# Two-block transformer kernel: differential queries and keys computed with tokens stationary and turned by VectorE and moves; which queues issue the moves

## The chip, the cores and the metric

The kernel runs on one core of a Trainium2 chip. The metric is the device time of one execution in microseconds; the median of three runs stands for the kernel.

## What is computed

The reference chains two layers over 256 tokens of 2048 channels, all in float32: a sliding-window attention layer, and a layer with a latent attention branch (MLA, 16 heads), a differential attention branch (8 heads, two 128-wide query/key pairs each), gates for both, and a gated feed-forward network. The change is in the differential branch:

```
dq, dk, dv = columns of h @ w_in                       # 2048 columns each
q = dq.reshape(b, s, 8, 2, 128); k likewise; v = dv.reshape(b, s, 8, 256)
sc = einsum('bqhmd,bkhmd->bhmqk', q, k) / sqrt(128) - slope_h * |i - j|   # chunk mask of 64
p = softmax(sc);  a = p[:, :, 0] - lam * p[:, :, 1]
o = rmsnorm(einsum('bhqk,bkhd->bqhd', a, v)) * (1 - lambda_init)
merged = g0 * (y_mla @ w_mla_proj) + g1 * (o @ w_diff_proj)
x = x + merged @ w_out;   then   x = x + (silu(h2 @ w_gate) * (h2 @ w_up)) @ w_down
```

## The kernel before

All weights lie in one array `w` of 340 chunks of 1 MB, in the order in which they are used: a chunk is 16 weight tiles of 128 x 128. SyncE (SP) loads them in that order into four buffers `w_raw` (line 54). Every half chunk is split into a high and a low part of type float32r: ScalarE (ACT) casts the high one (`w_hi`, line 85), VectorE (DVE) subtracts (`w_lo`, line 86), four buffers each. Activations are split in the same way. A product is then three float32r products: high x high, high x low, low x high. All matmuls are issued by `mm` (line 209).

There are two forms of the big products. `gemm` (line 330) holds a weight tile stationary and sends activations through: `w_hi` against the 512 columns (high and low) of one k, `w_lo` against the 256 high ones; the result has channels on partitions. `gemm_nat` (line 389) holds 128 tokens stationary and sends four weight tiles through: for each k and each of two token halves `nat3` (line 378) issues three matmuls of 512 columns; the result has tokens on partitions, in two PSUM banks.

The differential branch is a loop over u = 0 to 3, two heads each (lines 977 to 996). In a step, eight blocks of `gemm("dqk", ...)` make four blocks of queries and four of keys, channels on partitions; each is summed from its PSUM halves and scaled by `scaled` (line 420: one ScalarE copy, two VectorE operations of 128 x 256). `gemm_nat("dv", ...)` makes the values. Then `attend_d` (line 919) is put into an interleaver. In step 0 the gates 0 to 3 and the `mla` projections follow; after the loop come the gates 4 to 7, `diff`, `out`, the feed-forward products `ffn` and `down`, all by `gemm_nat`.

The interleaver (lines 127 to 168) sets where attention stands in program order. The big products report the tiles that they have taken; after `every` tiles there is a tick, and a tick advances one generator up to its next `yield n`, which says after how many ticks it may go on (`apart` if it says nothing). During the differential loop from u = 0's end, `every` is 8 and `apart` 3; from the gates' end on `every` is 16. Program order is what the framework's list scheduler starts from; on each engine the instructions then run in one fixed order, and an instruction that waits holds up all behind it.

Some tensors are turned (transposed) without TensorE. VectorE transposes blocks of 32 x 32 (`nc.vector.transpose`), and `moved` (line 447) carries the blocks between partition groups with 16 small DMAs, four for each of four column groups `a`. Their issuing engine is GpSimd (POOL) unless a `queue` is given; with `fourth` given, the four of `a == 3` go to that queue. Before the change, the moves of probabilities (`prob_t`, line 468) have `fourth=nc.sync`; those of the turned outputs (`o_t`, line 917), of the merged, and of the ffn activations (`turned`, line 456) are all GpSimd's, as are the loads of the gates' bias rows (`row`, line 487, from line 950); the moves of the residual (`x1n`, lines 965 to 974) are all SyncE's. `split_turned` (line 471) makes the high and low copies of turned activations on ScalarE and VectorE, 5 ticks after it is first advanced.

Weight columns for results that will be turned are permuted on the host by `_quarters` (line 1153), so that after the 32 x 32 transposes and moves the channels stand in order.

Of the kernel before, what the change touches and what calls it, by code (L numbers as in the profile page):

```python
# [171 lines left out]
def block_kernel(ctx, tc, order, w, x01, xt, bc, rw, cst, out):  # L172
# [29 lines left out]
    def half(t, i):  # L202
        return t[:, (i % 2) * S:(i % 2) * S + S]
# [217 lines left out]
        total(o, ps)  # L421
        tt(o, o, rb, ALU.mult)

    def scores(parts, ps):

        n = len(parts)
        for j, (q, k) in enumerate(parts):
            mm(ps[:, 0:P], q[:, 0:P], k[:, 0:P], j == 0, False)
        for j, (q, k) in enumerate(parts):
            mm(ps[:, P:384], q[:, P:S], k[:, 0:S], False, j == n - 1)  # L430

    def exps(ps, table, scale, negmax, sums, init, rows=None):

        t = unit("prob")[:, 0:384]
# [18 lines left out]
                    out=o[32 * b:32 * b + 32, a * n:a * n + n], in_=tr[32 * a:32 * a + 32, b * n:b * n + n])  # L453
        return o

    def turned(z, queue=nc.gpsimd):

        tr = unit("turn")
        nc.vector.transpose(out=tr, in_=z)  # L459
        return moved(tr, unit("turned"), queue)  # L460

    def turned_probs(p):

# [4 lines left out]
        d = moved(tr, wide("prob_t"), fourth=nc.sync).rearrange("p (a e k i) -> p e k a i", a=4, e=2, k=3)  # L468
        return [d[:, e] for e in range(2)]

    def split_turned(acts, k0, parts):

        yield 5
        hls = []
        for t in parts:
            t = t.rearrange("p (a g i) -> p g a i", a=4, g=4)
            make = unit2 if acts is act and k0 < 8 else unit
            hi, lo = make("t_hi", F32R), make("t_lo", F32R)
            oh, ol = (o.rearrange("p (g a i) -> p g a i", a=4, g=4) for o in (hi, lo))
            nc.scalar.copy(out=oh, in_=t)  # L480
            tt(ol, t, oh.bitcast(F32), ALU.subtract)
            hls.append((hi, lo))
        for g in range(4):
            q = slice(g * P, g * P + P)
            acts[k0 + g] = [(hi[:, q], lo[:, q]) for hi, lo in hls]
# [383 lines left out]
    tab_d = unit("tab_d")[:, 0:384]  # L869
    nc.scalar.dma_start(out=tab_d, in_=cst[:, C_DD:C_DD + 384])  # L870

    def probs_d(head, q, k):
        negmax, sums, rec = sm("negmax"), sm("sums"), sm("rec")
        slope = 2.0 ** -(head + 1)
        bias = unit("bias")[:, 0:384]
        nc.scalar.activation(out=bias, in_=tab_d, func=AF.Copy, scale=slope / scale_d)
        p = []
        for m in range(2):
            ps = bank("s")
            scores([(half(q, m), half(k, m))], ps)  # L880
            p.append(exps(ps, bias, scale_d, negmax[:, 2 * m:2 * m + 2], sums[:, 2 * m:2 * m + 2], BIG))
        nc.vector.reciprocal(out=rec, in_=sums)
        nc.vector.tensor_scalar(out=rec[:, 2:4], in0=rec[:, 2:4], scalar1=neglam, scalar2=None, op0=ALU.mult)
        for qb, (a, b) in enumerate(((0, P), (P, 384))):
            nc.scalar.activation(out=p[1][:, a:b], in_=p[1][:, a:b], func=AF.Copy, scale=rec[:, 2 + qb:3 + qb])
            nc.vector.scalar_tensor_tensor(out=p[0][:, a:b], in0=p[0][:, a:b], scalar=rec[:, qb:qb + 1],
                                           in1=p[1][:, a:b], op0=ALU.mult, op1=ALU.add)
        return p[0]
# [20 lines left out]
    def turned_values(o, r):  # L909

        tr = unit("o_tr")
        to = tr.rearrange("p (b d q i) -> p q d b i", b=4, d=2, q=2)
        for qb in range(2):
            nc.vector.tensor_scalar(out=half(o, qb), in0=half(o, qb), scalar1=r[:, qb:qb + 1], scalar2=None,
                                    op0=ALU.mult)
            nc.vector.transpose(out=to[:, qb], in_=half(o, qb).rearrange("p (d b j) -> p d b j", d=2, b=4))
        return moved(tr, unit("o_t"))

    def attend_d(u, q, k, v):
        heads = (2 * u, 2 * u + 1)  # L920
        p = []
        for e, head in enumerate(heads):
            p.append(probs_d(head, q[e], k[e]))
            yield
        pts = turned_probs(p)
        yield 9
        ms = sm("ms_d")
        os = []
        for e in range(2):
            os.append(values_d(pts[e], [(half(a, e), half(b, e)) for a, b in v], ms[:, 2 * e:2 * e + 2]))  # L930
            yield
        r = rstd(ms, S)
        yield
        ots = [turned_values(o, r[:, 2 * e:2 * e + 2]) for e, o in enumerate(os)]
        for e, head in enumerate(heads):
            yield 8
            ot = ots[e].rearrange("p (a d q i) -> p d q a i", a=4, d=2, q=2)
            for d in range(2):
                y = unit(f"y_d{2 * head + d}", F32R)
                g = g_d[:, d:d + 1]  # L940
                for tb in range(2):
                    hi, lo = (half(y, i)[:, tb * P:tb * P + P].rearrange("p (a i) -> p a i", a=4) for i in range(2))
                    nc.scalar.activation(out=hi, in_=ot[:, d, tb], func=AF.Copy, scale=g)
                    nc.vector.scalar_tensor_tensor(out=lo, in0=ot[:, d, tb], scalar=g, in1=hi.bitcast(F32),
                                                   op0=ALU.mult, op1=ALU.subtract)
                y_d[2 * head + d] = y

    def gate(i):

        b = row(R_GATE, i)  # L950
        o = []
        for tb, ps in enumerate(gemm_nat("gate", i * 512, h)):
            t = unit("gate")
            nc.vector.scalar_tensor_tensor(out=t, in0=ps, scalar=r_2[:, tb:tb + 1], in1=b, op0=ALU.mult, op1=ALU.add)
            nc.scalar.activation(out=t, in_=t, func=AF.Tanh, scale=0.5)
            o.append(t)
        return o
# [7 lines left out]
    def turn_residual():  # L965
        for cb in range(4):
            for tb in range(2):
                yield 8
                tr = unit("turn")
                for i in range(4):  # L970
                    nc.vector.transpose(
                        out=tr.rearrange("p (a m j) -> p a m j", a=4, m=4)[:, :, i, :],
                        in_=x1[4 * cb + i][:, tb * P:tb * P + P].rearrange("p (a j) -> p a j", a=4))
                x1n.append(moved(tr, unit("x1n"), nc.sync))

    mer = []
    for u in range(4):
        qk = []
        for c in (0, 16):
            for i in range(4):  # L980
                ps = gemm("dqk", c + 4 * u + i, h)
                if i % 2 == 0:
                    qk.append(unit("qk_d"))
                scaled(half(qk[-1], i), ps, rb_2)
        pp = gemm_nat("dv", u * 512, h)
        v = []
        for tb in range(2):
# [5 lines left out]
        if u == 0:  # L993
            between.drain()
            between.every, between.apart = 8, 3
        between.add(attend_d(u, qk[0:2], qk[2:4], v))
        if u == 0:
            between.add(turn_residual())
            for i in range(4):
# [51 lines left out]
    for u in range(KF // 4):  # L1051
# [11 lines left out]
            pu = gemm_nat("ffn", DFF + u * 512, h)  # L1063
        for tb, ps in enumerate(pu):
            tt(parts[tb], ps, parts[tb], ALU.mult)
            parts[tb] = turned(parts[tb])
        between.add(split_turned(act, 4 * u, parts))

    tot = sm("tot", 10)
    fgt = []  # L1070
# [91 lines left out]
def _matrices(i):  # L1162

    pairs = []
    for j in range(16):
# [11 lines left out]
        "out_a": i["w_out_a"][0][pairs],  # L1177
        "in_2": in_2[:, :1280],
        "kpe": np.concatenate([kpe, kpe], axis=1),
        "dqk": in_2[:, 1344:5440],  # L1180
        "dv": in_2[:, 5440:7488],
        "gate": in_2[:, 7488:][:, _quarters(2 * D)],
        "uq": np.concatenate([uq[:, :, :128].reshape(768, -1), uq[:, :, 128:].reshape(768, -1)], axis=1),
# [44 lines left out]
```

## Time and profile before

| | |
|---|---|
| time, median of 3 runs | 1982.64 us (1982.47 to 1982.7) |
| the profiled execution | 1981.54 us |
| its span, first to last instruction | 1979.8 us |
| mean granted TensorE clock | 0.998 |
| ScalarE, VectorE busy | 997.5 us, 1247.0 us |
| DMA, mean over the span | 199 GB/s |

In the rows below, a line of a timeline has the start in us, the duration in us, engine, line of the kernel, operation, output tile <- input tiles, shape, number of instructions merged, and in brackets how long the engine idled before it and what ended that. POOLq and SPq are the issuing sequencers. Rows by tile have durations in ns (least, median, most) and the first and last start. Rows of DMA issues end with the median us from issue to landing. Matmul records overlap, since TensorE is pipelined; the pitch is read from the starts.

### The profile page before, as it was taken

Reading aid. Unit: us, or ns where it says so; the run is one execution under the profiler, and the core shown is the slowest. Engines: PE = TensorE matmul, PEld = TensorE weight load, DVE = VectorE, ACT = ScalarE, POOL = GpSimd, SP = SyncE. Lnnn points to the kernel's source line nnn. Section 1 sums busy time; section 2 is a strip of 40 time slices with the busy share of each in tenths; the row PEclk is TensorE's granted clock in tenths of the full one; section 3 lists DMA queues with packets and bytes.
Section 4 is the critical chain, followed back from the end, with each engine's and each line's share of the span. In section 5 each row is a group of like instructions: output and inputs, shape, how many; then the busy total and the mean of one; then the engine's idle time right before and its main releaser. Section 6 shows DMA issues by size and latency. Waiting matters only on the chain. (4 is left out here: it accounts for less than half of the span.)

```text
span 1979.8 us, 27202 instructions
## 1 busy us (share of the span) xinstructions
PE 1960.2 (99%) x9756; PEld 1648.5 (83%) x9756; DVE 1247.0 (63%) x1960; ACT 997.5 (50%) x1577; POOL 526.9 (27%) x1069
## 2 busy tenths in 40 slices
PE   9999999999999999999999999999999999999998
PEld 8888888888888888888888888887888888888886
DVE  7889766888856655566666666655555555544453
ACT  6677664756645444455554445544444444434443
POOL 0555200014311300014043565433444333330000
PEclk9999999999999999999999999999999999999999
DMA  8565554445455555555556665655556565565552
GB/s 304 186 211 190 187 212 160 173 152 197 159 202 198 170 222 223 198 180 186 200 200 229 210 215 190 238 208 194 207 207 210 204 211 204 202 224 192 193 192 105
DMA packets 100793, 393.16 MB, mean 199 GB/s; under 512 B 27248, under 2 KB 53104, under 8 KB 57520
## 3 DMA queue, kind: packets, MB, share of 16 engines
q1 hardware_dynamic: 65184, 366.17, 51.4%
q0 software_dynamic: 34320, 23.27, 4.2%
q10 hardware_dynamic: 1152, 1.97, 0.3%
q8 instruction: 77, 1.26, 0.3%
q14 instruction: 60, 0.49, 0.1%
HBM read 364.03 MB, written 2.10 MB: 185 GB/s over the span
## 5 line engine op out<-in xcount | busy, mean ns | idle before, releaser
L86 DVE TENSOR_TENSOR w_lo<-w_raw,w_hi 128x1024 fp32r<-128x1024 f32 (+1 forms) x677 | 821.2, 1218 | 556.8 <-ACT w_hi L85 552.3
L85 ACT CAST w_hi<-w_raw 128x1024 fp32r<-128x1024 f32 (+1 forms) x677 | 705.0, 1046 | 707.3 <-PE ps_g L209 632.5
L209 PE MATMUL ps_g<-w_lo,t_hi 128*128 128x512 f32 x1176 | 457.6, 389 | 0.8 <-DVE w_lo L86 0.8
L209 PE MATMUL ps_g<-w_hi,t_hi 128*128 128x512 f32 x1176 | 457.6, 389 | 0.6 <-ACT w_hi L85 0.6
L209 PE MATMUL ps_g<-w_hi,t_lo 128*128 128x512 f32 x1176 | 457.4, 389 | 0.0
L452 POOL DMA_DIRECT2D turned<-turn x576 | 281.7, 497 | 394.5 <-DVE turn L459 169.5
L209 PE MATMUL ps_g<-h,w_hi 128*128 128x512 f32 x1160 | 283.7, 393 | 3.1 <-ACT w_hi L85 2.8
L452 POOL DMA_DIRECT2D prob_t<-prob_tr x336 | 164.7, 498 | 397.5 <-DVE prob_tr L467 274.2
L209 PEld LDWEIGHTS ps_g<-w_hi,t_hi 128*128 128x128 f32 x1176 | 220.8, 188 | 46.8 <-ACT w_hi L85 1.0
L209 PEld LDWEIGHTS ps_g<-w_lo,t_hi 128*128 128x128 f32 x1176 | 220.8, 188 | 46.6 <-DVE w_lo L86 1.1
L209 PEld LDWEIGHTS ps_g<-w_hi,t_lo 128*128 128x128 f32 x1176 | 220.8, 188 | 45.9
L209 PEld LDWEIGHTS ps_g<-h,w_hi 128*128 128x128 f32 x1160 | 212.0, 188 | 47.8 <-ACT w_hi L85 3.4
L209 PE MATMUL ps_g<-w_hi,h 128*128 128x512 f32 x768 | 240.9, 391 | 0.0
L209 PEld LDWEIGHTS ps_g<-w_hi,h 128*128 128x128 f32 x768 | 144.2, 188 | 29.9
L209 PEld LDWEIGHTS ps_g<-h,w_lo 128*128 128x128 f32 x1160 | 150.2, 191 | 9.7 <-issue 3.0
L209 PE MATMUL ps_g<-h,w_lo 128*128 128x256 f32 x1160 | 155.2, 284 | 0.0
L209 PE MATMUL ps_g<-w_lo,h 128*128 128x512 f32 x384 | 149.7, 390 | 0.9 <-DVE w_lo L86 0.7
L290 POOL TENSOR_TENSOR rstd<-ms,mhalf 128x2 f32<-128x2 f32 (+1 forms) x10 | 9.2, 920 | 358.6 <-DVE ms L285 341.0
L209 PEld LDWEIGHTS ps_g<-w_lo,h 128*128 128x128 f32 x384 | 72.1, 188 | 16.2 <-DVE w_lo L86 1.6
L452 POOL DMA_DIRECT2D o_t<-o_tr x128 | 62.8, 498 | 63.0 <-issue 24.8
L209 PE MATMUL ps_g<-w_hi,y_m 128*128 128x512 f32 x256 | 79.5, 389 | 0.0
L209 PE MATMUL ps_g<-w_hi,y_d 128*128 128x512 f32 x256 | 78.9, 389 | 0.0
(240 smaller groups left out, 1799.6 us busy)
## 6 DMA issues: line engine op xcount, KB each, us to landing
w_raw<-w SPq DMA_DIRECT2D x337, 1024.0 KB, 5.0
turned<-turn POOLq DMA_DIRECT2D x576, 16.0 KB, 4.0
prob_t<-prob_tr POOLq DMA_DIRECT2D x336, 24.0 KB, 3.6
row<-rw POOLq DMA_DIRECT2D x12, 256.0 KB, 3.7
prob_t<-prob_tr SPq DMA_DIRECT2D x112, 24.0 KB, 2.9
w_raw<-w SPq DMA_DIRECT2D x5, 512.0 KB, 7.6
x1n<-turn SPq DMA_DIRECT2D x128, 16.0 KB, 1.8
o_t<-o_tr POOLq DMA_DIRECT2D x128, 16.0 KB, 3.8
```

Of the source, the lines that this page charges most:

```text
L85: a = nc.scalar.copy(out=hi[:, q], in_=src[:, q])
L86: b = nc.vector.tensor_tensor(out=lo[:, q], in0=src[:, q], in1=hi.bitcast(F32)[:, q], op=ALU.subtract)
L209: nc.tensor.matmul(out=o, lhsT=a, rhs=b, start=start, stop=stop, skip_group_check=True)
L290: nc.gpsimd.tensor_tensor(out=r, in0=t, in1=mhalf[:, 0:n], op=ALU.pow)
L452: (fourth if fourth and a == 3 else queue).dma_start(out=o[32 * b:32 * b + 32, a * n:a * n + n], in_=tr[32 * a:32 * a + 32, b * n:b * n + n])
```

## The change

Queries and keys of the differential branch are computed by `gemm_nat`, four weight tiles of one k at a time, and evicted by one scaled ScalarE copy per token half. Each 128 x 512 result is turned by VectorE and 16 moves, of which 4 go to SyncE. A new function `dense_d`, run as the first part of `attend_d`, copies the turned queries and keys on ScalarE into the layout that the scores read. The helper `scores` goes; its two products per pair are written out in `probs_d`. The ticks of `attend_d` are set anew: 2, 1, 2, 1, 8, 1, 1, 1, 8, 1 in place of 3, 3, 9, 3, 3, 3, 8, 8.

The moves of `o_t` and of the ffn activations also give a fourth to SyncE. Those of `x1n`, before all on SyncE, go three quarters to GpSimd. The bias rows of the gates are loaded by SyncE. In the ffn, `split_turned` waits 7 ticks in place of 5. The columns of `dqk` are permuted by `_quarters`.

```diff
-    def turned(z, queue=nc.gpsimd):
+    def turned(z, queue=nc.gpsimd, fourth=None):
         tr = unit("turn")
         nc.vector.transpose(out=tr, in_=z)
-        return moved(tr, unit("turned"), queue)
+        return moved(tr, unit("turned"), queue, fourth)
...
-    def split_turned(acts, k0, parts):
-        yield 5
+    def split_turned(acts, k0, parts, wait=5):
+        yield wait
...
-    def probs_d(head, q, k):
+    def dense_d(q, k):
+        qs, ks = [], [unit("k_d") for _ in range(2)]
+        for tb in range(2):
+            t = unit("q_d")
+            nc.scalar.copy(out=t.rearrange("p (g a i) -> p g a i", a=4, g=4),
+                           in_=q[tb].rearrange("p (a g i) -> p g a i", a=4, g=4))
+            qs.append(t)
+            for e in range(2):
+                nc.scalar.copy(out=ks[e].rearrange("p (g t a i) -> p t g a i", g=2, t=2, a=4)[:, tb],
+                               in_=k[tb].rearrange("p (a g i) -> p g a i", a=4, g=4)[:, 2 * e:2 * e + 2])
+        return qs, ks
+
+    def probs_d(head, e, qs, ks):
...
             ps = bank("s")
-            scores([(half(q, m), half(k, m))], ps)
+            qm = [q[:, (2 * e + m) * P:(2 * e + m) * P + P] for q in qs]
+            mm(ps[:, 0:P], qm[0], ks[e][:, m * S:m * S + P], True, False)
+            mm(ps[:, P:384], qm[1], half(ks[e], m), False, True)
...
-        return moved(tr, unit("o_t"))
+        return moved(tr, unit("o_t"), fourth=nc.sync)
 
     def attend_d(u, q, k, v):
         heads = (2 * u, 2 * u + 1)
+        yield 2
+        qs, ks = dense_d(q, k)
+        yield 1
         p = []
         for e, head in enumerate(heads):
-            p.append(probs_d(head, q[e], k[e]))
-            yield
+            p.append(probs_d(head, e, qs, ks))
+            yield 2 - e
         pts = turned_probs(p)
-        yield 9
+        yield 8
...
-            yield
+            yield 1
         r = rstd(ms, S)
-        yield
+        yield 1
         ots = [turned_values(o, r[:, 2 * e:2 * e + 2]) for e, o in enumerate(os)]
         for e, head in enumerate(heads):
-            yield 8
+            yield 1 if e else 8
...
-        b = row(R_GATE, i)
+        b = row(R_GATE, i, nc.sync)
...
-                x1n.append(moved(tr, unit("x1n"), nc.sync))
+                x1n.append(moved(tr, unit("x1n"), fourth=nc.sync))
...
         for c in (0, 16):
-            for i in range(4):
-                ps = gemm("dqk", c + 4 * u + i, h)
-                if i % 2 == 0:
-                    qk.append(unit("qk_d"))
-                scaled(half(qk[-1], i), ps, rb_2)
+            parts = []
+            for tb, ps in enumerate(gemm_nat("dqk", (c + 4 * u) * P, h)):
+                z = unit("qk_d")
+                nc.scalar.activation(out=z, in_=ps, func=AF.Copy, scale=r_2[:, tb:tb + 1])
+                parts.append(turned(z, fourth=nc.sync))
+            qk.append(parts)
...
-        between.add(attend_d(u, qk[0:2], qk[2:4], v))
+        between.add(attend_d(u, qk[0], qk[1], v))
...
-            parts[tb] = turned(parts[tb])
-        between.add(split_turned(act, 4 * u, parts))
+            parts[tb] = turned(parts[tb], fourth=nc.sync)
+        between.add(split_turned(act, 4 * u, parts, 7))
...
-        "dqk": in_2[:, 1344:5440],
+        "dqk": in_2[:, 1344:5440][:, _quarters(2 * D)],
```

More of the change, by code (lines that the diff above doesn't have):

```diff
@@ L422, in scaled @@
         tt(o, o, rb, ALU.mult)
[L424 to L430, printed above, removed]
     def exps(ps, table, scale, negmax, sums, init, rows=None):
```

## The prediction

> **What bounds the kernel now.** I read the page first, then the chain of waits in order of time, then the timelines of TensorE, ScalarE, SyncE and GpSimd around the places where TensorE idled, and last the rows by tile for durations. Page and chain:
>
> ```profile
> span 1979.8 us, 27202 instructions
> PE 1960.2 (99%) x9756; PEld 1648.5 (83%) x9756; DVE 1247.0 (63%) x1960; ACT 997.5 (50%) x1577; POOL 526.9 (27%) x1069
> ...
> 1368.55 595.77 PE ps_g L209 x2627
> ```
>
> The span is TensorE's: 99% busy, and the last 596 us of the chain are one unbroken run of matmuls. That run is made by `gemm_nat` alone, 512 columns each, so one of these costs 595.77 / 2627 = 226.8 ns from start to start. Every other engine has room on the average. So the change can act in two ways: by another number of nanoseconds of matmul, and by stalls of TensorE that go or come. Vector, scalar and move work that causes no stall costs nothing.
>
> **Matmul time.** The rewritten part is the 32 blocks of `gemm("dqk", ...)`, 16 weight tiles each. In TensorE's timeline one block reads:
>
> ```profile
> 783.33 3.82 PE L209 MATMUL ps_g<-h,w_hi 128*128 128x512 f32 x16
> 786.99 2.08 PE L209 MATMUL ps_g<-h,w_lo 128*128 128x256 f32 x16
> 788.90 3.82 PE L209 MATMUL ps_g<-h,w_hi 128*128 128x512 f32 x16
> ```
>
> The starts matter, not the durations, which overlap: 16 matmuls of 512 columns take 786.99 - 783.33 = 3.66 us (228.8 ns each), 16 of 256 take 788.90 - 786.99 = 1.91 us (119.4 ns), a block 5.57 us (5.565 over two blocks, by the starts). [...] With tokens stationary, `gemm_nat` sends the same columns as 96 matmuls of 512 for four blocks (6 for each of 16 k), where there were 64 of 512 and 64 of 256. That is 24 x 226.8 ns = 5.44 us a block. The gain is 0.12 us a block, times 32 = 3.9 us.
>
> [...]
>
> The scores are the same four products per head with the same widths, so I cost them at zero; they are now issued inside the same streams as before.
>
> **Stalls of TensorE that the change touches.** From the dqk blocks on, TensorE's timeline shows idle time before four matmuls, at three places:
>
> ```profile
> 779.47 2.11 PE L209 MATMUL ps_g<-h,w_hi 128*128 128x512 f32 x8 [2.24 <-ACT w_hi L85]
> ...
> 1024.46 0.50 PE L209 MATMUL ps_g<-w_lo,h 128*128 128x512 f32 x1 [0.73 <-DVE w_lo L86]
> ...
> 1367.29 0.49 PE L209 MATMUL ps_g<-w_hi,t_hi 128*128 128x512 f32 x1 [0.58 <-ACT w_hi L85]
> 1368.55 0.50 PE L209 MATMUL ps_g<-w_lo,t_hi 128*128 128x512 f32 x1 [0.77 <-DVE w_lo L86]
> ```
>
> They add to 4.32 us. The record of a matmul lasts longer (0.39) than its pitch (0.227), which hides 0.16 us of each: 4 x 0.16 = 0.65, together 5.0 us. In each the weights' split came late; why, the other engines show:
>
> ```profile
> 751.68 21.50 SPq L452 DMA_DIRECT2D x1n<-turn  x32
> 773.28 15.09 SPq L54 DMA_DIRECT2D w_raw<-w  x7
> ...
> 778.38 2.00 ACT L85 CAST w_hi<-w_raw 128x1024 fp32r<-128x1024 f32 x2 [11.06 <-DMA w_raw<-w]
> ...
> 1021.68 0.51 ACT L894 CAST a_hi<-prob_t 128x384 fp32r<-128x384 f32 x1 [7.91 <-DMA row<-rw]
> ...
> 1355.36 0.62 ACT L480 CAST t_hi<-turned 128x512 fp32r<-128x512 f32 x1 [6.60 <-DMA turned<-turn]
> ...
> 1364.52 0.62 ACT L480 CAST t_hi<-turned 128x512 fp32r<-128x512 f32 x1 [5.69 <-DMA turned<-turn]
> ```
>
> First: SyncE issued 32 moves of `x1n` in one run of 21.5 us; the weight loads stood behind them. Now three quarters go to GpSimd and 8 of such 32 stay on SyncE, a run of about 5.4 us. As 21.5 us overran the weights' lead by only 2.4 us, the lead is about 19 us and 5.4 us is covered. Second: ScalarE stood 7.9 us at the copy of turned probabilities. Third: it stood at the copies of turned ffn activations (6.6 and 5.7 us). A ScalarE wait blocks the casts of weights queued behind it, and TensorE runs dry when the wait exceeds ScalarE's lead: 7.91 us of wait cost 0.73 + 0.16 = 0.9 us, so the lead is about 7.0 us. For the second place GpSimd's timeline says what was slow:
>
> ```profile
> 1010.18 3.91 POOL L452 DMA_DIRECT2D prob_t<-prob_tr  x8 [1.05 <-DMA o_t<-o_tr]
> 1015.08 1.96 POOL L452 DMA_DIRECT2D prob_t<-prob_tr  x4 [0.99 <-DMA prob_t<-prob_tr]
> 1017.03 1.09 POOL L490 DMA_DIRECT2D row<-rw  x2
> ...
> 1056.11 4.43 POOL L452 DMA_DIRECT2D o_t<-o_tr  x9 [9.31 <-issue]
> ...
> 1072.78 2.94 POOL L452 DMA_DIRECT2D o_t<-o_tr  x6 [1.41 <-DMA o_t<-o_tr]
> ```
>
> The probabilities queued behind `o_t` moves and ahead of bias rows. A long run of moves also waits for its own landings: 32 moves of `o_t` took 1075.72 - 1056.11 = 19.6 us, 0.61 us each. After the change a run of 32 is 24 on GpSimd, 14.7 us, and the bias rows are off its queue. The ffn copies wait 7 ticks of 16 tiles instead of 5: two ticks are 2 x 24 x 226.8 ns = 10.9 us more, above the 5.7 us by which they were late. I take all 5.0 us as gone; at the least it is the first alone, 2.4 us.
>
> **The other terms, and what hides them.**
>
> ```profile
> L417 ACT COPY qk_d<-ps_g x32: 348/372/379, 520.1 to 958.8; 128x256 f32<-128x256 f32 x32
> L212 DVE TENSOR_TENSOR qk_d<-qk_d,ps_g x32: 383/420/422, 520.5 to 959.2; 128x256 f32<-128x256 f32 x32
> L212 DVE TENSOR_TENSOR qk_d<-qk_d,rb_kr x32: 382/425/426, 521.4 to 959.6; 128x256 f32<-128x256 f32 x32
> ...
> L989 ACT ACTIVATE v_hi<-ps_g,r x8: 687/689/691, 590.2 to 982.7; 128x512 fp32r<-128x512 f32 x8
> ...
> L459 DVE STREAM_TRANSPOSE turn<-ffn x22: 701/703/706, 1294.0 to 1732.9; 128x512 f32<-128x512 f32 x22
> ...
> L480 ACT CAST t_hi<-turned x38: 611/618/624, 1128.3 to 1756.0; 128x512 fp32r<-128x512 f32 x38
> ...
> turned<-turn POOLq DMA_DIRECT2D x576, 16.0 KB, 4.0
> x1n<-turn SPq DMA_DIRECT2D x128, 16.0 KB, 1.8
> ...
> L452 SPq DMA_DIRECT2D x1n<-turn x128: 507/588/1729, 618.5 to 772.6; - x128
> ```
>
> VectorE loses 64 x 0.42 = 26.9 us and gains 16 transposes x 0.70 = 11.2 us: 15.7 us less. ScalarE loses 32 x 0.37 = 11.9 us and gains 16 x 0.69 = 11.0 us of scaled evictions, 8 copies of 512 at 0.62 and 16 of 256 at 0.37 = 10.9 us: 10 us more on an engine half idle. GpSimd gains 192 q/k and 96 `x1n` moves and loses 32 `o_t`, 88 ffn and 8 rows: +160, or 80 us at the 0.49 us of the unhindered rows (3.91 for 8). SyncE gains 64 + 32 + 88 + 8 and loses 96: +96 at 0.59 = 57 us. None of this lies on the path while the copies that need the moves come later than the landings.
>
> That is the one unknown. The attention of step u-1 runs in ticks of 8 tiles (12 x 226.8 ns = 2.72 us) beside q, k and v of step u, 24 ticks. The k moves are queued at tick 16.5 and need 24 x 0.61 = 14.7 us or 5.4 ticks, landing 4.0 us later at tick 23.4. `dense_d` copies them at tick 27 of the program, and ScalarE is there up to 7.0 us (2.6 ticks) early: 24.4. So they are just covered. The `o_t` moves (tick 18) stand behind the k moves and end at tick 27.3; their copies stand at ticks 26 and 27, so ScalarE can wait there. Bounds: nothing, if ScalarE's order puts the casts first or the moves go at 0.49 us (4.3 ticks each); at most, at the two steps where this happens (u = 2 and 3), the last landing at tick 28.8 against need at 27, 5 us and a cast's delay, 6 us each. Below nothing I exclude: the three stalls are already taken. I take 1.7 us, a third of the 5.0 us that three such waits cost here, as if one more came.
>
> **Sum.** The profiled execution took 1981.54 us, its span and 1.74 us around it; the median of the runs shown, 1982.64, is 1.1 us above. 1981.5 - 3.9 - 5.0 + 1.7 = 1974.3 us for a profiled execution, 1975.4 us for the median. A measurement here tells apart about 0.2%, 4 us.
>
> **Rivals.** *SyncE becomes the late one.* Its queue carries all weight loads and now more moves, each waiting for a VectorE transpose, and 8 bias rows that wait for a free one of 57 unit tiles, of which `h` (16), `x1n` (8), `mer` (8), the gates (8) and `y_d` (16) hold 56 at the end of the gates. For it: the 21.5 us run cost 2.4 us in just this way. Against: the new runs are 8 moves, and 19 us of lead cover their 5.4. If 2.4 us came back at two or three rows or moves, 1982.6 - 3.9 - 5.0 + 6 = 1979.7 us: no difference that can be told. 24%.
>
> *GpSimd falls behind, and it is slower.* If the `o_t` moves are issued in front of the k moves, or moves take over 0.61 us, `dense_d` waits as well: 5.4 ticks less the 1.0 of cover is 12 us, 5 us over ScalarE's lead, at steps 2 and 3, beside the 6 us each of the `o_t` copies: 22 us at most. 1982.6 - 8.9 + 22 = 1995.7; with two thirds of it, 1988. It decides from a backlog of one tick, 2.7 us. For it: 84 moves a step (48 of q and k, 12 of probabilities, 24 of `o_t`) at 0.61 us are 51 us of the step's 24 x 2.72 = 65. Against: the probabilities' copies waited past the lead only once in all of before. 14%.
>
> [...]
>
> *The new blocks cost as much as the old.* If a block's time went by its columns, which stay the same, the first term would be nothing: 1982.6 - 5.0 + 1.7 = 1979.3 us, no difference that can be told. Against it stand the 119.4 ns of half a width beside 226.8 ns over 2627 matmuls. 4%. [...]
>
> **How the numbers follow.** The forecast has 58%: 1973.7 (no new stall) to about 1978, at 1975.4. The low end of the range allows 1.5 us more for gaps that I have not seen, 1972; the high end reaches past the SyncE rival to 1985 and leaves out most of GpSimd's, some 12 in 100. Faster by over 4 us: 55 from the forecast and 5 from the SyncE rival, 60%. Same: 3 from the forecast, 19 from the SyncE rival, 4 from the last and 1 from GpSimd's, 27%. Slower: 13%.
>
> **What would show it.** Right: in place of the dqk blocks, runs of 512-column matmuls at 227 ns; no idle before the first matmuls of step 1; no ScalarE wait over 7 us for moves at the ffn's start; the span shorter by the two terms. Wrong: matmuls of the new blocks above 229 ns; ScalarE idle at `k_d`, `q_d`, `y_d` until a move lands, with TensorE's idle behind it; SyncE in front of late weight loads.

## The result, and the profile after

The changed kernel takes 1986.77 us (median; the kernel before, on the same chip, 1984.02 us). The ratio, formed without one execution of the kernel before that took 2164.49 us, is 1.0018, with a 95% interval of 1.0009 to 1.0026: slower by just under 0.2%, where 1975.4 us was forecast and the range ended at 1985. The executions of the changed kernel lie between 1984.81 and 1992.75 us, and the one in the profile, 1984.81 us, is the fastest of them; it is 3.27 us above the profiled execution of before.

The page of the kernel after, span and engines:

```profile
span 1983.0 us, 27321 instructions
PE 1959.2 (99%) x9500; PEld 1637.2 (83%) x9500; DVE 1231.9 (62%) x1912; ACT 1009.0 (51%) x1585; POOL 604.9 (31%) x1229
```

The loads of the engines moved as worked out: TensorE has 256 matmuls fewer, VectorE lost 15.1 us (15.7 forecast), ScalarE gained 11.5 (10), GpSimd gained 78 us (80). The time is therefore not in the work but in waits. To find them I cut the span at three places that both programs have: the first `dqk` matmul, the first matmul of `diff` (it reads `y_d`), and the last matmul. The first cut is at 514.38 us before and 514.28 after; the rows by tile give the second as the first start in each row (the first row is of before, the second of after):

```profile
L209 PE MATMUL ps_g<-w_hi,y_d x256: 389/389/390, 1075.5 to 1162.3; 128*128 128x512 f32 x128
```

```profile
L209 PE MATMUL ps_g<-w_hi,y_d x256: 389/389/389, 1077.4 to 1164.2; 128*128 128x512 f32 x128
```

| us, profiled execution | before | after | difference |
|---|---|---|---|
| A: first `dqk` matmul to first `diff` matmul | 561.13 | 563.15 | +2.02 |
| B: from there to the last matmul's start | 894.27 | 892.35 | -1.92 |
| C: from there to the end of the span | 9.99 | 13.18 | +3.19 |

B is the ffn's stall, gone as forecast; what removed it is looked at under the runs below. A should have become 5.5 us shorter (3.9 of matmul time and 3.3 of the first two stalls, less the 1.7 allowed for new waits) and became 2 us longer. C was not in the forecast at all.

**Stage A.** TensorE's timeline of the kernel after, from the dqk blocks on, all starts that came over 0.3 us late:

```profile
921.61 0.49 PE L209 MATMUL ps_s<-k_d,q_d 128*128 128x128 f32 x2 [2.18 <-ACT k_d L874]
922.74 1.35 PE L209 MATMUL ps_s<-k_d,q_d 128*128 128x256 f32 x6 [0.64 <-ACT k_d L874]
...
966.63 0.39 PE L209 MATMUL ps_t<-v_hi,a_hi 128*128 128x256 f32 x1 [0.36 <-ACT a_hi L902]
...
982.52 0.78 PE L209 MATMUL ps_g<-w_lo,h 128*128 128x512 f32 x1 [2.26 <-DVE w_lo L86]
983.10 1.05 PE L209 MATMUL ps_g<-w_hi,h 128*128 128x512 f32 x2
...
1002.93 0.50 PE L209 MATMUL ps_g<-w_lo,h 128*128 128x512 f32 x1 [0.76 <-DVE w_lo L86]
```

None of the three stalls of before is there: the run of `x1n` moves on SyncE is now 8 long, and no matmul waits at 779 us. In their place stand five late starts, 6.2 us together, and one thing more: after the gap at 980 us pairs of matmuls take 1.05 us instead of 0.62. A table of stretches (us, then busy time and count of TensorE, its weight loads, VectorE, ScalarE and GpSimd, then the granted clock, the DMA share and GB/s) shows why:

```profile
982.60:986.00 3.40, 3.40 (x8) 2.72 (x9) 3.40 (x5) 0.00 (x0) 3.40 (x8) 0.50 0.28 63
986.00:990.00 4.00, 4.00 (x19) 3.25 (x18) 1.19 (x2) 0.00 (x0) 3.58 (x8) 1.00 0.72 272
```

For 3.40 us TensorE had half its clock (0.50 in the table), which costs 1.7 us more. It followed the gap of 2.26 us at 980 us; the gap of 2.18 us at 921 us was not followed by it (1.00 from 921.5 to 930 us).

Who was late, ScalarE's timeline shows:

```profile
914.94 1.28 ACT L954 ACTIVATE y_d<-o_t,g_d 128x128 fp32r<-128x128 f32 x4 [5.29 <-DMA o_t<-o_tr]
...
919.46 1.28 ACT L954 ACTIVATE y_d<-o_t,g_d 128x128 fp32r<-128x128 f32 x4 [1.36 <-DMA o_t<-o_tr]
920.65 0.60 ACT L870 COPY q_d<-turned 128x512 f32<-128x512 f32 x1
921.15 0.71 ACT L874 COPY k_d<-turned 128x256 f32<-128x256 f32 x2
...
991.24 1.28 ACT L954 ACTIVATE y_d<-o_t,g_d 128x128 fp32r<-128x128 f32 x4 [9.55 <-DMA o_t<-o_tr]
992.42 1.99 ACT L85 CAST w_hi<-w_raw 128x1024 fp32r<-128x1024 f32 x2
```

These are the waits that the prediction named: the `y_d` copies of steps 2 and 3 stand at `o_t` moves. Behind them, in ScalarE's fixed order, stand the copies of `q_d` and `k_d` (so the scores at 921 us were late) and casts of weights. The gap at 980 us is another thing, which the prediction had not seen. VectorE's timeline, and then GpSimd's:

```profile
971.15 0.19 DVE L285 TENSOR_SCALAR ms<-ms_d 128x4 f32<-128x4 f32 x1
978.88 0.62 DVE L922 TENSOR_SCALAR o_d<-o_d,rstd 128x256 f32<-128x256 f32 x2 [7.54 <-POOL rstd L290]
...
981.28 3.46 DVE L86 TENSOR_TENSOR w_lo<-w_raw,w_hi 128x1024 fp32r<-128x1024 f32 x3
```

```profile
970.88 3.91 POOL L444 DMA_DIRECT2D turned<-turn  x8 [1.47 <-DMA turned<-turn]
976.33 1.47 POOL L444 DMA_DIRECT2D turned<-turn  x3 [1.54 <-DMA turned<-turn]
977.81 1.03 POOL L290 TENSOR_TENSOR rstd<-ms,mhalf 128x4 f32<-128x4 f32 x1
980.72 5.93 POOL L444 DMA_DIRECT2D o_t<-o_tr  x12 [1.87 <-ACT v_hi L1001]
```

The values are normalised by a power, `rstd`, that runs on GpSimd. Its input was ready at 971.3 us; GpSimd was issuing moves of `k`, and came to it at 977.81. VectorE stood for 7.54 us, with three remainders of weights (`w_lo`) behind it, and TensorE ran dry. The `o_t` moves, too, could begin only after it.

**Stage C.** Rows of the kernel's last line, the sequencers' drains (count, ns least, median, most, first and last start); first before, then after:

```profile
L1215 POOLq DRAIN  x3: 46/93/7624, 1971.4 to 1979.5; - x3
L1215 SPq DRAIN  x3: 7/7/116, 1977.6 to 1979.2; - x3
```

```profile
L1227 POOLq DRAIN  x3: 46/98/10809, 1971.4 to 1982.7; - x3
L1227 SPq DRAIN  x3: 7/7/7, 1977.5 to 1982.4; - x3
```

In both programs GpSimd begins its drain at 1971.4 us and SyncE has seen the last output at 1977.6. GpSimd's drain lasted 7.62 us before, and 10.81 after. The span ends when it is over, so the 3.2 us of C are its. The number of DMAs that GpSimd issues went from 1053 to 1213.

### The profile page after: what moved, and what is told of

Same layout as the page of the kernel before. It is cut to its first block, busy times and chain, and to the rows that moved or that the text cites. A ratio compares the mean times of both kernels' runs of the same rounds, so it can differ in the third digit from the quotient of the medians.

```text
span 1983.0 us, 27321 instructions
## 1 busy us (share of the span) xinstructions
PE 1959.2 (99%) x9500; PEld 1637.2 (83%) x9500; DVE 1231.9 (62%) x1912; ACT 1009.0 (51%) x1585; POOL 604.9 (31%) x1229
## 4 chain that ended last, share of the span: by engine, by line
PE 92%; DMA 3%; DVE 2%; POOL 1%; ACT 1%; issue 1%; SPq 0%; POOLq 0%; ACTq 0%; DVEq 0%
PE ps_g L209 86%; PE ps_s L209 4%; PE ps_t L209 2%; DMA turned<-turn 1%; DMA o_t<-o_tr 1%; POOL o_t L444 1%; DVE w_lo L86 0%; POOL turned L444 0%; ACT w_hi L85 0%; DMA w_raw<-w 0%; DVE rope_t L212 0%; DMA prob_t<-prob_tr 0%; DVE k_n L212 0%; POOL prob_t L444 0%; ACT prob L434 0%
## 5 line engine op out<-in xcount | busy, mean ns | idle before, releaser
L444 POOL DMA_DIRECT2D turned<-turn x680 | 332.7, 497 | 562.3 <-DVE turn L451 296.2
L209 PE MATMUL ps_g<-w_hi,h 128*128 128x512 f32 x1280 | 402.1, 392 | 0.0
L209 PEld LDWEIGHTS ps_g<-w_hi,h 128*128 128x128 f32 x1280 | 241.2, 188 | 50.9 <-issue 0.3
L209 PE MATMUL ps_g<-w_lo,h 128*128 128x512 f32 x640 | 250.1, 391 | 3.0 <-DVE w_lo L86 3.0
L209 PE MATMUL ps_g<-h,w_hi 128*128 128x512 f32 x648 | 160.0, 394 | 0.0
L209 PEld LDWEIGHTS ps_g<-w_lo,h 128*128 128x128 f32 x640 | 120.6, 188 | 28.4 <-DVE w_lo L86 3.8
L209 PEld LDWEIGHTS ps_g<-h,w_hi 128*128 128x128 f32 x648 | 117.9, 188 | 25.3 <-issue 2.3
L209 PEld LDWEIGHTS ps_g<-h,w_lo 128*128 128x128 f32 x648 | 84.7, 191 | 7.3 <-issue 2.7
L209 PE MATMUL ps_g<-h,w_lo 128*128 128x256 f32 x648 | 88.2, 284 | 0.1
```

The source lines that it names most:

```text
L209: nc.tensor.matmul(out=o, lhsT=a, rhs=b, start=start, stop=stop, skip_group_check=True)
L444: (fourth if fourth and a == 3 else queue).dma_start(out=o[32 * b:32 * b + 32, a * n:a * n + n], in_=tr[32 * a:32 * a + 32, b * n:b * n + n])
```

## The experiments

The theory from the two traces: the matmul term and the removed stalls came as forecast; stage A gave them back through waits on GpSimd's queue; and the end grew with GpSimd's DMAs. The rivals: that the new blocks are no cheaper, that the moved DMAs disturb, and that the end has another cause than GpSimd's DMAs. The results in one table (medians; ratio to the kernel before on the same chip; stages of the profiled execution):

| kernel | us | ratio, 95% interval | A | C | GpSimd DMAs | drain, us |
|---|---|---|---|---|---|---|
| before | 1984.02 | | 561.1 | 10.0 | 1053 | 7.62 |
| after | 1986.77 | 1.0018 (1.0009 to 1.0026) | 563.2 | 13.2 | 1213 | 10.81 |
| yd_later | 1975.79 | 0.9962 (0.9949 to 0.9975) | 554.1 | 13.2 | 1213 | 10.81 |
| queues_only | 1974.64 | 0.9959 (0.9944 to 0.9973) | 557.2 | 8.9 | 1021 | 5.01 |
| qk_only | 2002.51 | 1.0096 (1.0079 to 1.0113) | 586.6 | 8.6 | 1245 | 3.54 |
| pad_before | 2031.32 | 1.0245 (1.0229 to 1.0260) | | | 1209 | 10.48 |
| n1253 | 1971.66 | 0.9931 (0.9914 to 0.9947) | 554.1 | 8.6 | 1253 | 4.19 |
| n1237 | 1971.21 | 0.9930 (0.9915 to 0.9945) | 554.1 | 8.6 | 1237 | 2.89 |
| after_n1237 | 1982.01 | 0.9986 (0.9975 to 0.9998) | 565.7 | 8.6 | 1237 | 2.89 |
| qk_half_sp | 1982.95 | 0.9993 (0.9983 to 1.0002) | 564.9 | 8.6 | 1149 | 5.58 |
| half_later | 1972.20 | 0.9937 (0.9922 to 0.9952) | 554.7 | 8.6 | 1149 | 5.58 |
| ot_first | 2000.89 | 1.0083 (1.0066 to 1.0100) | 579.5 | 13.2 | 1213 | 10.81 |
| rstd_on_vector | 1984.78 | 1.0011 (1.0002 to 1.0021) | 562.0 | 13.2 | 1213 | 10.81 |

**The `y_d` copies later** (in `attend_d`, nothing else):

```diff
         for e, head in enumerate(heads):
-            yield 1 if e else 8
+            yield 2 if e else 11
```

> The changed kernel with one edit: the copies of turned differential outputs (y_d) wait 11 and 2 ticks in place of 8 and 1. Theory 1 (ScalarE stands at the y_d copies because the o_t moves queue behind the k moves on GpSimd; this starves the weight casts): the changed kernel loses 8.7 us of TensorE between 919 and 1003 us of its span (2.3 + 0.7 + 0.5 + 2.4 + 1.0 us of starts that come late, and 1.75 us in a stretch at half the granted clock). With the copies 8 us later they go, the last matmul starts at about 1961 us in place of 1969.8, and the time falls from 1986.8 to about 1978 us. Rival 1 (the waits only move to the next copy): same time within 2 us. Theory 2 (the end: GpSimd's last wait is longer the more DMAs it has issued): its last drain stays at about 10.8 us.

Two numbers of ticks give 11 us. ScalarE's timeline of this kernel at step 3 has the copies of queries and keys and four casts ahead of the `y_d` copies, and these wait for nothing (the one wait left there, 3.89 us at a `q_d` copy, is within the lead of about 7 us that the prediction estimated for ScalarE, and no late matmul follows it):

```profile
983.21 0.71 ACT L874 COPY k_d<-turned 128x256 f32<-128x256 f32 x2
983.82 0.52 ACT L882 ACTIVATE bias<-tab_d 128x384 f32<-128x384 f32 x1
984.25 3.87 ACT L85 CAST w_hi<-w_raw 128x1024 fp32r<-128x1024 f32 x4
...
990.01 0.68 ACT L954 ACTIVATE y_d<-o_t,g_d 128x128 fp32r<-128x128 f32 x2
```

Stage A falls from 563.2 to 554.1 us with no start of a matmul over 0.3 us late in it; by the two profiled executions the new waits had cost 9.1 us. (By the medians it is 11 us; after's profiled execution is the fastest of its 17.) VectorE's longest wait for `rstd` is 2.82 us here, and no late matmul follows it: the 24 moves of `k` took 13.4 us, with pauses of 1.4 us in all, where those of after took some 16 us with pauses of 4.1 us. C stays at 13.2 us, so the end is a matter by itself.

**The queues alone** (before, with every edit of the change that only names a queue, and the ffn's 7 ticks; queries and keys as before):

```diff
-        return moved(tr, unit("o_t"))
+        return moved(tr, unit("o_t"), fourth=nc.sync)
...
-        b = row(R_GATE, i)
+        b = row(R_GATE, i, nc.sync)
...
-                x1n.append(moved(tr, unit("x1n"), nc.sync))
+                x1n.append(moved(tr, unit("x1n"), fourth=nc.sync))
...
-            parts[tb] = turned(parts[tb])
-        between.add(split_turned(act, 4 * u, parts))
+            parts[tb] = turned(parts[tb], fourth=nc.sync)
+        between.add(split_turned(act, 4 * u, parts, 7))
```

> The kernel before with the moves' queues alone: a fourth of o_t and of the ffn's moves to SyncE, three fourths of x1n to GpSimd, the bias rows to SyncE, ffn copies after 7 ticks; queries and keys as before. Theory 1: nothing stands in front of the o_t moves, the three stalls of before (2.4, 0.9 and 1.8 us) go and no new one comes: 5 us faster than before, about 1979 us. Theory 2: GpSimd issues 1021 DMAs, 32 fewer than before, so its last drain is as before, 7 to 7.6 us. Rival 2 (SyncE becomes late with moves and rows in its queue): late weight loads, no gain over before.

A falls by 4.0 us and B by 1.9 us: the three stalls of before were worth 5.9 us (5.0 forecast), and all go. Their removal needs nothing of the new queries and keys. With it stands the matmul term: the two kernels without late starts, this one and yd_later, differ in stage A by 557.2 - 554.1 = 3.1 us, the worth of the 32 blocks (3.9 forecast). GpSimd's drain, 5.01 us with 1021 DMAs, is shorter than the 7 to 7.6 us expected.

**Queries and keys alone** (after, with these edits undone):

```diff
-        return moved(tr, unit("o_t"), fourth=nc.sync)
+        return moved(tr, unit("o_t"))
...
-        b = row(R_GATE, i, nc.sync)
+        b = row(R_GATE, i)
...
-                x1n.append(moved(tr, unit("x1n"), fourth=nc.sync))
+                x1n.append(moved(tr, unit("x1n"), nc.sync))
...
-            parts[tb] = turned(parts[tb], fourth=nc.sync)
-        between.add(split_turned(act, 4 * u, parts, 7))
+            parts[tb] = turned(parts[tb])
+        between.add(split_turned(act, 4 * u, parts))
```

> The changed kernel with the queues of before: o_t, ffn moves and bias rows on GpSimd alone, x1n on SyncE alone, ffn copies after 5 ticks; only queries and keys with tokens stationary and their turning are kept. Theory 1: the o_t moves on GpSimd are 32 in place of 24 behind the k moves, so the y_d copies come 8 x 0.61 = 4.9 us later at two steps, and the three stalls of before come back: about 10 us slower than the changed kernel, 1997 us. Theory 2: GpSimd issues 1245 DMAs in place of before's 1053, its last drain takes about 11.5 us in place of 7.6. Rival 3 (the new blocks' matmuls cost as much as the old): pitch above 229 ns in them; theory 1 has 227.

With these edits undone stage A is 23 us longer than in after. TensorE's timeline:

```profile
700.74 0.59 PE L209 MATMUL ps_g<-w_hi,h 128*128 128x512 f32 x1 [3.85 <-ACT w_hi L85]
...
941.30 1.22 PE L209 MATMUL ps_s<-k_d,q_d 128*128 128x128 f32 x4 [9.22 <-ACT k_d L874]
...
1022.49 0.80 PE L209 MATMUL ps_s<-k_d,q_d 128*128 128x128 f32 x2 [7.22 <-ACT k_d L874]
```

The scores wait 9.2 and 7.2 us for `k_d`, whose copies stand on ScalarE behind `y_d` copies that waited for `o_t` moves (7.71 and 5.31 us at step 2, 2.62 and 7.31 us at step 3). With each of the two waits the clock halves for 10.2 us, some of it spent in the wait itself (means of 0.68 from 934 to 941 us, 0.50 from 941 to 945 and 0.56 from 945 to 947; 0.75 from 1015 to 1022, 0.50 from 1022 to 1028 and 0.83 from 1028 to 1030). The weights come 3.85 us late at 700 us, behind a run of 32 `x1n` moves on SyncE (20.5 us) as in before, again with half clock (0.79 on the mean from 697 to 704 us). So the new queries and keys do worse without these edits; the edits were undone together, and their shares of the 23 us are not separated.

Two things came otherwise than expected. The ffn's stall did not come back: B is 892.35 us here, too, though the ffn's moves are all GpSimd's and its copies wait 5 ticks, as in before. So no run shows that the change's two edits in the ffn removed that stall. And the drain is 3.54 us with 1245 DMAs, where 11.5 us was expected: that it grows with every DMA is out.

**DMAs added to GpSimd** (before, with 156 moves that write a tile that nothing reads; work added):

```diff
+    pad = const.tile([P, 32], F32, name="pad")
+    for j in range(156):
+        nc.gpsimd.dma_start(out=pad[32 * (j % 4):32 * (j % 4) + 32],
+                            in_=ident[32 * (j % 4):32 * (j % 4) + 32, 0:32])
```

> The kernel before with 156 further small DMAs (32 partitions x 128 B, into a tile that nothing reads) on GpSimd's queue during the last product, where GpSimd is idle. Theory 2: GpSimd then issues 1209 DMAs, as many as in the changed kernel, and its last drain takes 10.8 us in place of 7.6, the time 3.2 us more than before's, with the last matmul at 1969.8 us as in before. Rival 4 (the length of the drain has to do with something else, or with chance): 7.6 us or any length, no difference in time. Theory 1 says nothing of this.

They were meant for the last stage, but the scheduler issued them early, where they delayed the first products; its time says nothing. The drain does: 10.48 us with 1209 DMAs, in a kernel with the queries and keys of before.

**A few more GpSimd DMAs** (yd_later, with SyncE's quarter of the ffn's moves taken back for some u: above 4 in n1253, above 2 in n1237):

```diff
-            parts[tb] = turned(parts[tb], fourth=nc.sync)
+            parts[tb] = turned(parts[tb], fourth=nc.sync if u > 2 else None)
```

> The changed kernel with the y_d copies later (11 and 2 ticks), and in the ffn the first five u without a fourth on SyncE: 40 more moves on GpSimd, 1253 DMAs in place of 1213. Theory 2 in a second form (the last drain of GpSimd goes by its number of DMAs, 0.0816 us each, and starts anew every 121, which fits the five lengths seen: 5.0 at 1021, 7.6 at 1053, 10.5 at 1209, 10.8 at 1213, 3.5 at 1245): 8 DMAs after a new start, drain 4.2 us, hidden behind SyncE's wait for the output (6.3 us after the drain's start); the span ends 4.5 us earlier than at 1213, 1971.3 us, with the last matmul at 1960.4. Rival 4 (the length is chance or the amount of work): 10.8 us or more, and 1975.8 us.

> As n1253, but with the first three u of the ffn without a fourth on SyncE: 24 more moves on GpSimd, 1237 DMAs. Theory 2 in its second form: 113 DMAs after a new start, drain 12.8 us, the span 2.0 us longer than at 1213, 1977.8 us, though only 16 DMAs differ from n1253, which should be 6.5 us faster. Rival 4: the same as n1253 within 1 us.

The expectations go by a second form of the theory, fitted to the five lengths known by then: the length grows by 0.0816 us a DMA and starts anew every 121. Again the drain became shorter with more DMAs. That of n1253 came as worked out, 4.19 us; that of n1237 did not, 2.89 us where 12.8 was expected: if the lengths start anew, they do so between 1213 and 1237 DMAs, not above them. Drains of n1237:

```profile
L1227 POOLq DRAIN  x3: 46/98/2886, 1962.3 to 1969.0; - x3
L1227 SPq DRAIN  x3: 7/7/7, 1968.5 to 1968.8; - x3
```

GpSimd is done at 1965.2, SyncE sees the last output at 1968.5, and the drain is hidden: C is 8.6 us instead of 13.2. At 1971.21 us n1237 has the lowest median here, 0.70% below before (0.9930, 0.9915 to 0.9945); n1253 and half_later (below) are not told apart from it.

**The same against after itself** (after, with the diff of n1237 alone):

> The changed kernel with its own ticks, and the first three u of the ffn without a fourth on SyncE: GpSimd issues 1237 DMAs in place of 1213, nothing else moves before the ffn. Theory 2 (the number of GpSimd's DMAs sets its last drain): drain 2.9 us as in n1237, hidden, so the span ends about 8.6 us after the last matmul in place of 13.2, and the time is 4.5 us under the changed kernel's, 1982 us; TensorE's late starts between 919 and 1003 us stay. Rival 4 (chance, or the later y_d copies made the end shorter): 1986.8 us.

4.8 us under after by the medians, where C gives 13.2 - 8.6 = 4.6. So the loss at the end goes while that of stage A stays. The profiled execution, 1984.48 us, is slower than this kernel's median: its stage A, 565.7 us, has the same kinds of late starts as after and two spells of half clock (pairs of matmuls take 1.05 us in place of 0.62 from 982.6 us on, and the six score matmuls at 1002 us take 2.07 us where after's at 922 us take 1.35), and B is 894.0 us, with a matmul 0.76 us late at 1277 us in the ffn (n1253 has one 0.55 us late, and B 893.3). Ahead of the ffn the edit changes nothing, so the 2.5 us between 565.7 and after's 563.2 are a spread between executions. Differences of this size in stage A, between kernels whose matmuls start late, say nothing by themselves.

**Half of the q and k moves by SyncE** (after; `moved` sends the column groups `a >= start` to the second queue):

```diff
-                parts.append(turned(z, fourth=nc.sync))
+                parts.append(turned(z, fourth=nc.sync, start=2))
```

> The changed kernel with two fourths of the query and key moves on SyncE in place of one, ticks as in the changed kernel: 16 k moves on GpSimd in place of 24, 1149 DMAs in all. Theory 1 (GpSimd's queue: the k moves stand before the root of the normalisation, which is GpSimd's too, and before the o_t moves): the o_t moves start 8 x 0.61 = 4.9 us earlier at steps 2 and 3, ScalarE's waits of 9.5 and 5.3 us at the y_d copies fall to under 5, below its lead of 7 us, and TensorE's 9 us of new stalls go; the last matmul starts at about 1961 us. Theory 2, second form: drain 5.6 us, hidden, so about 1972 us. Rival 5 (the waits come of the ticks alone, not of GpSimd's queue): stalls as in the changed kernel, last matmul at 1969 us. Rival 2 (SyncE late): new waits of the casts for weights.

Stage A did not become shorter: 564.9 us, within that spread of after's 563.2. GpSimd's timeline, then ScalarE's:

```profile
971.62 1.03 POOL L290 TENSOR_TENSOR rstd<-ms,mhalf 128x4 f32<-128x4 f32 x1
974.53 3.98 POOL L444 DMA_DIRECT2D o_t<-o_tr  x8 [1.87 <-issue]
...
985.37 3.91 POOL L444 DMA_DIRECT2D o_t<-o_tr  x8 [2.64 <-issue]
```

```profile
985.99 1.28 ACT L954 ACTIVATE y_d<-o_t,g_d 128x128 fp32r<-128x128 f32 x4 [2.02 <-DMA o_t<-o_tr]
993.41 1.28 ACT L954 ACTIVATE y_d<-o_t,g_d 128x128 fp32r<-128x128 f32 x4 [6.14 <-DMA o_t<-o_tr]
```

The power runs 6 us earlier than in after, and the gap at 980 us is gone. But the 24 `o_t` moves themselves take 17.5 us, 0.73 us each, and the `y_d` copies still wait 8.2 us in front of casts. TensorE idles 4.2 us until 998 us, and has half clock for 6.8 us, which begin within that gap (0.89 on the mean from 994 to 997 us, 0.50 from 997.8 to 1003). So the backlog of `k` moves is not all of it: with fewer of them ahead, the copies at ticks 26 and 27 still come before the `o_t` moves have landed. With the later ticks added:

> qk_half_sp with the y_d copies later too (11 and 2 ticks). Theory 1: both remedies remove the same stalls, so the last matmul starts at 1960.4 us as with the later copies alone; with theory 2's short drain about 1971.3 us. If SyncE's longer runs of moves delay weights, slower than that.

Stage A is 554.7 us, as with the later ticks alone. Once the copies come later, it does not matter who carries the `k` moves.

**The `o_t` moves ahead of the k moves** (after; the values are asked for 3 ticks earlier):

```diff
         pts = turned_probs(p)
-        yield 8
+        yield 5
```

> The changed kernel with one edit: the values are taken 5 ticks after the turned probabilities in place of 8, so that on GpSimd's queue the root of the normalisation and the 24 o_t moves stand before the 24 k moves; the distance of the y_d copies from the o_t moves stays 8 ticks. Theory 1 (the order on GpSimd's queue makes the y_d copies wait): no wait over 3 us at y_d, and instead the copies q_d and k_d may wait, since the k moves end at tick 25.8 and land at 27.3, where ScalarE would be at 24.4: up to 8 us of wait, 1 us over its lead; the last matmul at 1961 to 1964 us. Rival 5 (8 ticks are too few whatever stands in the queue): waits at y_d as in the changed kernel, last matmul at 1969 us. Theory 2: 1213 DMAs, drain 10.8 us.

This is the rival of the prediction in which GpSimd falls behind, made on purpose. It comes to 2000.9 us, above that rival's upper 1995.7, but only in part by that mechanism. The waits moved from `y_d` to `k_d`. ScalarE's timeline, then a line of TensorE's:

```profile
957.28 0.51 ACT L902 CAST a_hi<-prob_t 128x384 fp32r<-128x384 f32 x1 [5.87 <-DMA turned<-turn]
...
988.26 1.28 ACT L954 ACTIVATE y_d<-o_t,g_d 128x128 fp32r<-128x128 f32 x4 [2.36 <-DMA turned<-turn]
...
1002.52 0.40 ACT L874 COPY k_d<-turned 128x256 f32<-128x256 f32 x1 [5.74 <-DMA turned<-turn]
```

```profile
957.85 0.39 PE L209 MATMUL ps_t<-v_hi,a_hi 128*128 128x256 f32 x1 [4.81 <-ACT a_hi L902]
```

The waits at `k_d` and `q_d` cost TensorE late starts of 2.3 us at step 2 and 2.0 us at step 3, and no half clock (behind them the 512-column matmuls start 0.23 us apart). The larger part is another: 5 ticks after the probabilities their own moves have not landed, and TensorE waits 2.2, 4.8 and 4.7 us for `a_hi`, each time with half clock (3.4, 3.4 and 6.8 us; behind the first the 512-column matmuls start 0.43 us apart, the means are 0.60 and 0.59 from 957.8 to 962 us, and 0.50 from 1034.5 to 1040).

**VectorE's wait alone** (after; the scale of the values is a reciprocal on VectorE in place of the power on GpSimd, which leaves the root, the division by the width and the small constant out):

```diff
-        r = rstd(ms, S)
+        r = sm("rstd", 4)
+        nc.vector.reciprocal(out=r, in_=ms)
```

> The changed kernel, but the normalisation of the differential values is a plain reciprocal of the sums of squares on VectorE instead of the power on GpSimd; the scale of the values is therefore another one, and one small VectorE and one small GpSimd operation a step are left out. GpSimd's DMAs stay 1213, so all theories expect its last drain at 10.81 us. Theory A (new from the trace of the changed kernel: VectorE stood 7.54 us for the power, which GpSimd had queued behind the moves of k, and three remainders of weights stood behind VectorE's wait; this made TensorE's 2.26 us of idle time before the matmul at 982.5 us, and the 3.40 us at half clock after it): VectorE's waits for rstd in attend_d go, that late start and the half clock behind it go, about 4.1 us; the o_t moves of that step start up to 2.9 us earlier, so the y_d waits (9.55 and 2.31 us) become shorter by up to that much but do not go, and the late scores of step 2 (2.18 and 0.64 us) stay within 2 us. The first diff matmul to the first dqk matmul: 563.1 becomes 557 to 560; the median 1980 to 1984. Theory B (all new idle time comes from ScalarE's wait for the o_t moves, in front of casts): the late start near 980 stays at 2 us or more with the half clock behind it, and the stage stays within 1.5 us of 563; the median 1985 to 1988.

The gap at 980 us is gone, and its half clock with it, as theory A has it; the `y_d` wait of step 3 is 6.64 instead of 9.55 us. Yet A is 562.0 us, 1.2 us below after, which the spread between executions covers, and not the 3 to 6 us expected. TensorE's timeline shows what took the rest, and the table of stretches beside it:

```profile
922.88 0.79 PE L209 MATMUL ps_s<-k_d,q_d 128*128 128x128 f32 x2 [2.59 <-ACT k_d L874]
```

```profile
922.80:926.00 3.20, 2.79 (x9) 2.22 (x9) 0.35 (x1) 3.20 (x8) 0.00 (x0) 0.50 0.02 5
926.00:929.30 3.30, 3.30 (x10) 2.54 (x9) 3.30 (x7) 2.56 (x7) 0.00 (x0) 0.50 0.06 10
```

The wait of step 2 is 0.4 us longer, and now it is this one that half clock follows, for 6.8 us: some 3 us. What a gap of TensorE costs here is its length and in some cases half clock as well: 1.7 us behind the 2.26 us in after, some 3 us behind the 2.59 us here. The last section has the cases.

## Why the prediction was wrong, point by point

- **Matmul time: right.** 3.1 us measured, 3.9 forecast. The pitch of the new blocks is 227 ns. The case that the new blocks cost as much as the old is out. The measured gain is 97 ns a block, and the pitches in the prediction give as much: 16 matmuls of 256 columns at 119.4 ns take 96 ns more than 8 of 512 at 226.8 ns.
- **The three stalls of before: right in sum, the reason shown in part.** 5.9 us measured, 5.0 forecast. With the matmul time 9.0 us, against 8.9. That the run of `x1n` moves was the first stall's cause, qk_only bears out: there the run is back, and so is the late load. The forecast gave the ffn's stall to the two ticks more and the quarter on SyncE; qk_only has neither, and no stall. Why that stall went is open, and its 1.9 us of B may be luck. For the second stall, at the turned probabilities, no run tests the cause alone.
- **SyncE as the late one: did not happen.** The run of 8 `x1n` moves took 4.96 us (5.4 forecast), and no matmul of after waits for a load of weights.
- **The failed step: "I take 1.7 us, a third of the 5.0 us that three such waits cost here, as if one more came."** The waits were at the place and the steps that the prediction named, but cost 9.1 us in the profiled execution, inside its own bound of twice 6 us. The term was sized by stalls of other places, and three things were left out. GpSimd's queue carries not only moves: `rstd` stands behind the `k` moves, so the `o_t` moves begin later than the count of moves says, and VectorE waits with remainders of weights behind it (of after's late time, 2.4 us of gap and 1.7 us of half clock). The copies of `k_d` stand behind the `y_d` copies on ScalarE, so that scores wait as well as weights. And half clock followed a gap of TensorE, the 3.40 us at 0.50 behind the gap at 980 us. ScalarE's waits themselves, 5.29 and 1.36 us at step 2 and 9.55 and 2.31 us at step 3, were longer than the 5 us worked out for a step.
- **The missing term: the end.** The prediction counted GpSimd's 160 more DMAs as 80 us of hidden work. The hidden work was hidden; the drain behind it was not, 3.2 us.
- **The sum.** -3.1 - 5.9 + 9.1 + 3.2 = +3.3 us for the profiled execution, 3.27 measured. The terms are differences between the stages of four traces, so they must add up to this; that they do proves nothing more. Of the 11.4 us between forecast and median, the new waits are 7.4 and the end 3.2; the rest comes to 0.8 us, among it a median 1.96 us above the profiled execution, where 1.1 was taken.
- **GpSimd falls behind, 14%.** The kernel did become slower, but not by this mechanism: in after `dense_d` waits for no move of `k`. In ot_first `dense_d` waits as that rival has it; this cost 4.3 us of late starts, and most of the rest of its 2000.9 us came of `a_hi`.

Open: why the moves of `k` needed some 16 us at step 3 of after and 13.4 us in yd_later (the pauses, 4.1 and 1.4 us, make the difference, and the longer ones end with a landing of earlier moves), why the ffn's stall went, and what GpSimd does in its drain. The power itself on another engine was not tried.

## What to carry to other kernels

Before work is put on a queue that "has room", list everything that the engine does in its order, small operations too, and ask for each which engine waits for it and what stands behind that wait: here a 1 us power between moves stopped two engines. A copy of moved data belongs at a tick at which the landing is certain, with a margin: three to four ticks more for the consumers were worth 9.1 us here, and no later stage became longer. And look at the last 15 us of a span as a stage of its own.

## What was not expected of the hardware

- GpSimd's last drain had another length for each number of DMAs that GpSimd had issued in the whole kernel, and the same length for the same number (10.81 us with 1213 in after and in rstd_on_vector), though the last DMA of its queue, at 1747 us in after, lies far ahead of the drain at 1971 us. It took 10.48 and 10.81 us for 1209 and 1213 of them, 2.89, 3.54 and 4.19 us for 1237, 1245 and 1253: 0.082 us more for a DMA more within each group, and a shorter drain with 1237 than with 1213. By an estimate from all eight counts, with a period of 121 DMAs the 1021, 1053 and 1149 (5.01, 7.62 and 5.58 us) lie on the same line. That is a fit to eight counts, not a mechanism. In n1237 a drain of 2.89 us, begun at 1962.3, is hidden behind the last outputs, which SyncE sees 6.2 us later.
- TensorE's granted clock halved after 2.26 us of idle time at 980 us in after (0.50 from 982.60 to 986.00 us), after 2.59 us at 923 us in rstd_on_vector (0.50 from 922.8 to 929.3), after 1.87 us at 981 us in after_n1237 and behind its gaps of 1.66 and 0.64 us at 1001 and 1002 us; it stayed full after 2.24 us at 779 us in before (1.00 from 776.8 to 783) and after 2.18 us at 921 us in after (1.00 from 921.5 to 930). Lines of after_n1237, the second with the pair of matmuls at 1.05 us in place of 0.62:

```profile
981.42 0.50 PE L209 MATMUL ps_g<-w_lo,h 128*128 128x512 f32 x1 [1.87 <-DVE w_lo L86]
...
982.63 1.05 PE L209 MATMUL ps_g<-w_hi,h 128*128 128x512 f32 x2
```

- So a gap's length alone did not decide in these runs: 1.87 us was followed by half clock, 2.24 us was not. The spells of half clock lasted 3.4 us in after, 3.4, 3.4 and 6.8 us in ot_first, 6.8 us in qk_half_sp and rstd_on_vector and 10.2 us twice in qk_only. What decided besides the length, no run shows.
- The four slowest executions of after, 1989.55 to 1992.75 us, show a mean clock of 0.993 to 0.996, the four fastest one of 0.995 to 0.998. Whether half clock is what spreads them is not shown.
